# Attention scores as plain fp32 products on the two row halves of TensorE

## The chip, the cores and the metric

The kernel runs on one core of one Trainium2 chip. The metric is the device time in microseconds (us) of one execution; the time before is the median of three runs, 2792.22 us (2788.95 to 2793.67).

## What is computed

The reference is a trunk of two layers over 1024 latent tokens and 256 context tokens, 1024 channels wide, 16 heads of 64. Layer 0 mixes with a two-dimensional neighbourhood attention that has a learned relative-position bias; layer 1 with a sliding window (radius 128), four key-value heads for sixteen query heads, rotary positions and a sink logit for each head. In both a latent query sees its latent neighbours and all 256 context keys in one softmax. A gated convolutional feed-forward follows each. What matters here is the attention:

```
q = rmsnorm(q, g_q);  k = rmsnorm(k, g_k)          # per head of 64
s = einsum('...qngd,...knd->...ngqk', q, k) * 64 ** -0.5   # float32
s = s + bias   (layer 0)      or      where(mask, s, -1e30)   (layer 1)
s = concat([s, sink])         (layer 1)
o = einsum('...ngqk,...knd->...qngd', softmax(s), v)
x = x + gate * (o @ w_out)
```

Everything is fp32 at the inputs and the output.

## The kernel before

**Precision.** Most products run in the single-pass type fp32r. To keep accuracy an operand is split into a rounded part ("hi") and the rest ("lo"), and hi·hi, lo·hi and hi·lo are summed; this is how the projections (`mm`, `oacc`) and the feed-forward (`ua`, `uc`, `dn`) are computed. Products of probabilities and values (`pv`) and the transposes of probabilities (`pt<-idr,S`) are plain fp32.

**Stages.** The modulation and norms of layer 0 come first (to about 60 us), then attention of layer 0 (to about 640 us) with its output projection, then the feed-forward of layer 0 (about 790 to 1620 us), attention of layer 1 (about 1626 to 2060 us) with its projection, and the feed-forward of layer 1. The change touches the two attention stages.

**The order of the work.** Class `Sched` (line 61) is a planner that runs on the host. Each operation is put in with its engine (or a choice of two), an estimated duration, what it reads and writes, a key (smaller is more urgent) and the buffers that it takes (`acq`) and gives back (`rel`). The planner walks through time, gives each free engine its most urgent operation that is ready and whose buffers are free, and so fixes the order of issue on each engine; on the chip every engine then works through its list in that order. Buffers of a kind come free in the order in which they were taken. `CAPS` (line 1002) holds the number of each.

**Layer 0.** For each of 8 pairs of heads `plan_na_qkv` (line 1033) treats 10 tiles of 128 tokens, the two context tiles first: 24 products of 384 columns give queries, keys and values of both heads, which are normed; for each two tiles four plain transposes bring q and k of both heads, 128 rows by 512 columns, into one `pt` bank (line 1073). Then, head by head, 64 rows at a time, the split operands are built (lines 1083 to 1119): `qhi` and `khi` on ScalarE, `qlo` and `klo` on VectorE, and a copy of the keys' two parts to the other 64 rows. So 128 rows of the array hold for one head the query's hi on one half and its lo on the other, beside the same key part on both halves: one product over `kk` gives (hi+lo)·k_hi, a second over `kl` adds (hi+lo)·k_lo.

**Layer 1.** `plan_sw_qkv` (line 2176) does the same for 4 groups of four query heads and one key head: norm, rotary (`qa`, `qb`, `qs`), then the split (`kd`, `klo`, `qhi`, `qlo`, lines 2235 to 2255) into `st` and `klt`, two transposes of the key parts and four of the queries into `pt` banks, and their evacuations by ScalarE.

**Scores and softmax.** `plan_su` (line 571) treats two units of 128 queries: in layer 0 two query tiles of one head (called for head e = 0 and 1 with keys n and n + 1), in layer 1 two heads of one query tile. `qkc` puts the context scores of both units into one `s` bank, 256 columns each, with two products each; `qkl` puts the latent scores of one unit (256 or 384 columns) into another. VectorE reads the context part (`ctx_part`, negated, with a running minimum), then the latent part with bias or mask (`lat_part`); ScalarE takes the exponentials; VectorE or ScalarE scales; TensorE transposes the probabilities in blocks of 128 into `pt` banks, which are copied out. `plan_pv` (line 675) multiplies them with the values of two heads, one on each half of the array's columns, for all key blocks into one `pv` bank.

The eight PSUM banks of the attention stages are dealt out as `PSB = dict(s=3, pt=2, mm=2, pv=1)` (line 994). `Oproj` (line 793) is the output projection; `project` accumulates in `mm` banks, and `weights` loads and splits its weights.

Of the kernel before, what the change touches and what calls it, by code (L numbers as in the profile page):

```python
# [213 lines left out]
def trunk_kernel(ctx, tc, xperm, xseq, cc, crow, wmod, wmodt, bmod, gnorm, na_wqkv, na_gqk, na_bias, na_wo,  # L214
# [356 lines left out]
    def plan_su(sc, key, I, units, groups, psa, wk, reads):  # L571
# [12 lines left out]
        def qkl(k):  # L584
            nl = units[k]["nl"]

            def f(e):
                u = J["u", k]
                t = J["sl", k] = psa("s", F32)
                pe.matmul(t[:, :nl], u["q"], u["kk"], start=True, stop=False)  # L590
                pe.matmul(t[:, :nl], u["q"], u["kl"], start=False, stop=True)
            return f

        sc.op("pe", 4 * t_pe(256), qkc, reads=reads, writes=[K("sc")], key=key, acq=[("s", K("sc"), 2)],
              rel=units[0]["rel_c"] + units[1]["rel_c"])
        for k in range(2):
            if units[k]["nl"]:
                sc.op("pe", 2 * t_pe(units[k]["nl"]), qkl(k), reads=reads + [K("sc")], writes=[K("sl", k)], key=key,
                      acq=[("s", K("sl", k), 1)], rel=units[k]["rel_l"])
        for k in range(2):  # L600
            nl, sink = units[k]["nl"], units[k]["sink"]
            n = TC + nl

            def ctx_part(e, k=k):
                u = J["u", k]
# [4 lines left out]
                dve.tensor_scalar(out=J["S", k][:, :TC], in0=J["sc"][:, k * 256:k * 256 + 256], scalar1=-1.0,  # L610
                                  scalar2=u["sink"] if u["sink"] is not None else 3e38, op0=ALU.mult, op1=ALU.min,
                                  accum_out=J["m", k][:, 0:1])
            sc.op("dve", 0.36, ctx_part, reads=[K("sc")], writes=[K("Sc", k)], key=key,
                  acq=[("S", K("S", k), uses[k])], rel=[K("sc")])
            parts = [K("Sc", k)]
            if nl:
                def lat_part(e, k=k, nl=nl):
                    dve.tensor_tensor_reduce(out=J["S", k][:, TC:TC + nl], in0=J["sl", k][:, :nl], in1=J["u", k]["mask"],
                                             scale=-1.0, scalar=J["m", k][:, 0:1], op0=ALU.add, op1=ALU.min,
                                             accum_out=J["m", k][:, 1:2])  # L620
                sc.op("dve", 0.1 + nl * 0.0012, lat_part, reads=[K("sl", k), K("Sc", k)] + units[k]["mask_key"],
                      writes=[K("Sl", k)], key=key, rel=[K("sl", k)] + units[k]["mask_key"])
                parts.append(K("Sl", k))
# [51 lines left out]
    def plan_pv(sc, key, I, halves, psa, put, ok, acq):  # L675
# [7 lines left out]
        def mm(e):  # L683
            B["pv"] = psa("pv", F32)
# [11 lines left out]
        sc.op("pe", 0.25 + cols * 4 / 2400.0 + 0.02 * n, mm, reads=ps_ + vks, writes=[pk], key=key, acq=[("pv", pk, 1)], rel=ps_ + vks)  # L696
# [96 lines left out]
    class Oproj:  # L793
# [47 lines left out]
        def project(self, dt, key, parts, evac):  # L841

            sc, n = self.sc, self.n
            I = ("oa", dt)
            for kt in range(KT):
                def mm(e, kt=kt):
                    if kt == 0:
                        self.acc[dt] = self.psa("mm", F32)
                    ks = slice(kt * P, (kt + 1) * P)
                    hi, lo = self.ot[self.c]  # L850
                    for i, (w, o) in enumerate(((0, hi), (0, lo), (1, hi))):
                        pe.matmul(self.acc[dt][:, :n], self.w[dt][w][:, ks], o[:, kt, :], start=(kt == 0 and i == 0),
                                  stop=(kt == KT - 1 and i == 2))
                sc.op("pe", 3 * t_pe(n), mm, reads=[("woh", dt), ("wol", dt)] + parts[kt] + self.gate, writes=[I], key=key,
                      acq=[("mm", I, 1)] if kt == 0 else (), rel=[("wo", dt)])
# [138 lines left out]
    PSB = dict(s=3, pt=2, mm=2, pv=1)  # L994
# [6 lines left out]
    SBUFS, PTB = 5, dict(pt5=6, pt2=4, qsq=2)  # L1001
    CAPS = dict(PSB, raw=3, w=WBUFS, S=SBUFS, **PTB, qraw=2, qn=2, qa=2, qb=2, st=2, klt=2,
# [6 lines left out]
    kkl = fin.tile([P, 2, T], F32R, name="kkl")  # L1009
    kll = fin.tile([P, 2, T], F32R, name="kll")  # L1010
# [8 lines left out]
    sc = Sched(dict(CAPS, q=4, qc=1, crow0=1))  # L1019
# [13 lines left out]
    def plan_na_qkv(n):  # L1033
# [9 lines left out]
        def cp(e):  # L1043
            J["raw"] = wk.tile([P, 384], F32, tag="qraw", name="qraw", bufs=2)
# [17 lines left out]
        def qn(e):  # L1062
            if tt % 2 == 0:
                f["qn", pr] = wk.tile([P, 2, 256], F32, tag="qn", name="qn", bufs=2)
# [12 lines left out]
        sc.op("pe", 0.44, tr, reads=[two + (0,), two + (1,)], writes=[K("pt")], key=key, acq=[("pt", K("pt"), 8)], rel=[two])  # L1077
        kx = ("kkc", hp) if cx else ("kk", pr)
        kl = ("klc", hp) if cx else ("kl", pr)
        qx = ("q", hp, pr)  # L1080
        half = [slice(0, DH), slice(DH, P)]

        def qt():
            return f["q"][pr]

        def kt_(lo):
            return f["klc" if lo else "kkc"] if cx else (kll if lo else kkl)[:, :, (tt - 1) * P:(tt + 1) * P]

        def alloc():
            f["q"][pr] = fin.tile([P, 2, 256], F32R, tag="qc" if cx else "q", name="q", bufs=1 if cx else 4)  # L1090
            if cx:
                f["kkc"], f["klc"] = [fin.tile([P, 2, TC], F32R, tag=t, name=t, bufs=2) for t in ("kkc", "klc")]
        for x in range(2):
            a, b = half[x], half[1 - x]

            def qhi(e, x=x, a=a):
                if x == 0:
                    alloc()
                act.activation(qt()[a, x, :], J["pt"][a, 0:256], AF.Copy, scale=gg[a, 2:3])

            def khi(e, x=x, a=a):
                act.activation(kt_(0)[a, x, :], J["pt"][a, 256:512], AF.Copy)

            def qlo(e, x=x, a=a, b=b):
                dve.scalar_tensor_tensor(out=qt()[b, x, :], in0=J["pt"][a, 0:256], scalar=gg[a, 2:3],
                                         in1=qt()[a, x, :].bitcast(F32), op0=ALU.mult, op1=ALU.subtract)

            def klo(e, x=x, a=a):
                ENG[e].tensor_tensor(out=kt_(1)[a, x, :], in0=J["pt"][a, 256:512], in1=kt_(0)[a, x, :].bitcast(F32),
                                     op=ALU.subtract)  # L1110

            def other(lo):
                def f_(e, x=x, a=a, b=b):
                    copy(e, kt_(lo)[b, x, :], kt_(lo)[a, x, :].bitcast(F32))
                return f_
            first = [qx + (0, 0)] if x else []
            sc.op("act", t_actp(256), qhi, reads=[K("pt")] + first, writes=[qx + (x, 0)], key=key,
                  acq=([("qc" if cx else "q", qx, 4 if cx else 8)] + ([("kkc", kx, 20), ("klc", kl, 20)] if cx else []))
                  if x == 0 else (), rel=[K("pt")])
            sc.op("act", t_actp(256), khi, reads=[K("pt"), qx + (0, 0)], writes=[kx + (x, 0)], key=key, rel=[K("pt")])  # L1120
            both = [K("pt"), qx + (x, 0), kx + (x, 0)]
            sc.op("dve", t_dve(256), qlo, reads=both, writes=[qx + (x, 1)], key=key, rel=[K("pt")])
            sc.op("dve", t_dve(256), klo, reads=both, writes=[kl + (x, 0)], key=key, rel=[K("pt")])
            for lo, kk in ((0, kx), (1, kl)):
                sc.op(("act", "dve"), (t_act(256), 0.13 + 256 / 1920.0), other(lo), reads=[kk + (x, 0)], writes=[kk + (x, 1)],
                      key=key)
# [4 lines left out]
    def plan_na_su(n):  # L1131
# [4 lines left out]
        I = ("su0", hp, su, e)  # L1136
# [9 lines left out]
        reads = [t + (e, z) for t in (("kkc", hp), ("klc", hp), ("q", hp, su)) for z in range(2)]  # L1146
        for k in range(2):
# [3 lines left out]
            def get(tt=tt, ch=ch):  # L1151
                u = dict(q=f["q"][su][:, e, tt % 2 * P:(tt % 2 + 1) * P], kkc=f["kkc"][:, e, :], klc=f["klc"][:, e, :], sink=None)
                if tt < 8:
                    ks = slice(ch[0] * P, (ch[-1] + 1) * P)
                    u["kk"], u["kl"] = kkl[:, e, ks], kll[:, e, ks]
# [3 lines left out]
            units.append(dict(nl=len(ch) * P, sink=0, get=get, rel_c=[("q", hp, su), ("kkc", hp), ("klc", hp)],  # L1159
                              rel_l=[("q", hp, su)],  # L1160
                              mask_key=[("bias", hp, e, (0, 0, 1, 1, 1, 1, 2, 2)[tt])] if tt < 8 else []))
            reads += [(n, c // 2, e, z) for c in ch for n in ("kk", "kl") for z in range(2)]
# [17 lines left out]
        f["half", su, e] = plan_su(sc, key, I, units, groups, psa, wk, reads)  # L1180
# [53 lines left out]
    def plan_oproj0():  # L1234
# [12 lines left out]
        def evac(dt, I):  # L1247
            def load(e):
                xin[dt] = wk.tile([P, 384], F32, tag="qraw", name="cx", bufs=2)
# [918 lines left out]
    kkl1 = fin.tile([P, T], F32R, name="kkl1")  # L2168
# [350 lines left out]
```

## Time and profile before

| | |
|---|---|
| median of three runs | 2792.22 us |
| the profiled execution: its time, its span | 2790.61 us, 2788.8 us |
| granted clock of TensorE, mean | 0.990 |
| instructions | 43317 |
| fp32r score products (`s`) | 1088 |
| value products (`pv`), instructions | 1376 |
| transposes of probabilities (`pt<-idr,S`) | 1280 |
| transposes of split queries and keys in layer 1 (`st`, `klt`) | 208 |

In the rows of the profile PE is TensorE's products, PEld its weight loads, DVE VectorE, ACT ScalarE, POOL GpSimd and SP the queue of DMAs. A row of a group has the line, engine, operation, what is written and read, the shapes, the count, then the busy time in us with the mean in ns, and the idle time before the group's instructions with what ended it. All of the kernel's instructions go through one recording helper, so that every row says L51, and the names of the tiles tell the groups apart. `128*64` is the part of the array used, rows by columns. A row of the order in time has the start, the length, the operation and how many were merged. The products are pipelined and their ends modelled: a row's length holds some 0.17 us of latency, and what a product costs its successor is the distance of the starts.

### The profile page before, as it was taken

How to read it: one execution, taken by the hardware profiler on the slowest of the kernel's cores; microseconds unless marked ns; L12 is line 12 of the kernel's file. 1: busy time of each engine (PE TensorE's matmuls, PEld its weight loads, DVE VectorE, ACT ScalarE, POOL GpSimd, SP SyncE). 2: the span in 40 equal slices, each digit the busy share in tenths (PEclk: the TensorE clock that was granted, in tenths of full speed). 3: DMA queues.
4: the chain of work that ended last, by engine and by line, in shares of the span. 5: the costliest groups of instructions: out<-in, count | busy, mean ns of one | idle time of the engine just before them, and what ended most of it. 6: DMA issues, size and time to landing. Idle time of an engine off the chain costs nothing.

```text
span 2788.8 us, 43317 instructions
## 1 busy us (share of the span) xinstructions
PE 2710.8 (97%) x15496; PEld 2331.8 (84%) x15496; DVE 2290.1 (82%) x5040; ACT 1703.7 (61%) x3111; POOL 383.1 (14%) x550
## 2 busy tenths in 40 slices
PE   6999999998999999999999999999998999999999
PEld 4899999987799988888888888888877788888887
DVE  7888888887788788778886889889968988888767
ACT  5677777776455555656564557677754666566433
POOL 2111111112000000000010035656620000000000
PEclk9999999999999999999999999999999999999999
DMA  7233343325555543333475642223243223324655
GB/s 259 85 124 121 118 134 112 112 97 171 209 174 187 175 147 118 113 129 121 151 243 169 205 138 64 75 87 105 88 152 106 80 102 110 106 92 158 232 171 188
DMA packets 148463, 385.30 MB, mean 138 GB/s; under 512 B 21396, under 2 KB 34196, under 8 KB 147864
## 3 DMA queue, kind: packets, MB, share of 16 engines
q1 hardware_dynamic: 148248, 382.55, 41.3%
q8 instruction: 121, 1.98, 0.3%
q14 instruction: 94, 0.77, 0.1%
HBM read 315.50 MB, written 66.99 MB: 137 GB/s over the span
## 4 chain that ended last, share of the span: by engine, by line
PE 83%; DVE 6%; issue 3%; POOL 2%; ACT 1%; DMA 1%; POOLq 0%; DVEq 0%; ACTq 0%
PE ua L51 17%; PE dn L51 15%; PE mm L51 15%; PE uc L51 13%; PE pt L51 5%; PE pv L51 5%; PE s L51 4%; PE ud L51 4%; PE oacc L51 3%; PE dnc L51 2%; DVE S L51 1%; DVE wlo L51 1%; DVE x L51 1%; POOL qa L51 0%; ACT S L51 0%
## 5 line engine op out<-in xcount | busy, mean ns | idle before, releaser
L51 ACT ACTIVATE whi<-wraw 128x512 fp32r<-128x512 f32 (+1 forms) x264 | 212.0, 803 | 152.8 <-PE uc L51 57.4
L51 DVE TENSOR_TENSOR wlo<-wraw,whi 128x512 fp32r<-128x512 f32 (+1 forms) x264 | 240.7, 912 | 47.3 <-ACT whi L51 46.8
L51 ACT ACTIVATE S<-S,m 128x640 f32<-128x640 f32 (+3 forms) x288 | 221.0, 768 | 57.7 <-DVE m L51 39.3
L51 PE MATMUL dn<-ghi,whi 128*128 128x512 f32 x616 | 240.2, 390 | 0.0
L51 PE MATMUL dn<-ghi,wlo 128*128 128x512 f32 x616 | 239.9, 390 | 0.0
L51 PE MATMUL dn<-glo,whi 128*128 128x512 f32 x616 | 239.9, 389 | 0.0
L51 ACT ACTIVATE whi<-s 128x1024 fp32r<-128x1024 f32 (+1 forms) x120 | 113.2, 943 | 193.0 <-PE uc L51 117.9
L51 POOL TENSOR_TENSOR qy<-qv,mhalf 128x4 f32<-128x4 f32 (+2 forms) x120 | 136.7, 1139 | 546.4 <-DVE qv L51 512.7
L51 PE MATMUL pt<-idr,S 128*128 128x128 f32 x1280 | 189.8, 277 | 7.8 <-DVE S L51 3.3
L51 ACT ACTIVATE ghi<-graw 128x512 fp32r<-128x512 f32 x154 | 96.0, 629 | 150.3 <-PE dn L51 96.2
L51 PE MATMUL mm<-whi,h0hi 128*128 128x384 f32 x512 | 181.0, 354 | 1.6 <-ACT qraw L51 1.6
L51 PEld LDWEIGHTS pt<-idr,S 128*128 128x128 f32 x1280 | 151.6, 142 | 26.9 <-issue 9.9
L51 PE MATMUL mm<-wlo,h0hi 128*128 128x384 f32 x512 | 172.7, 337 | 0.0
L51 DVE TENSOR_TENSOR glo<-graw,ghi 128x512 fp32r<-128x512 f32 x154 | 106.2, 698 | 81.0 <-ACT ghi L51 48.4
L51 ACT ACTIVATE pt<-pt 128x512 f32<-128x512 f32 (+2 forms) x241 | 124.5, 536 | 56.6 <-PE pt L51 55.1
L51 PE MATMUL pv<-pt,v 128*64 128x256 f32 (+1 forms) x1376 | 154.7, 371 | 0.0
L51 DVE TENSOR_TENSOR wlo<-s,whi 128x1024 fp32r<-128x1024 f32 (+1 forms) x120 | 129.8, 1081 | 23.3 <-ACT whi L51 23.0
L51 PE MATMUL ua<-t12hi,whi 128*128 128x512 f32 x352 | 139.1, 395 | 4.9 <-ACT t12hi L51 4.7
L51 PE MATMUL uc<-t34h,whi 128*128 128x512 f32 x352 | 139.7, 397 | 0.5 <-ACT t34h L51 0.5
L51 PE MATMUL ua<-t12lo,whi 128*128 128x512 f32 x352 | 138.6, 394 | 1.4 <-DVE t12lo L51 1.4
L51 PE MATMUL uc<-t34l,whi 128*128 128x512 f32 x352 | 137.9, 392 | 0.9 <-DVE t34l L51 0.9
L51 PE MATMUL ua<-t12hi,wlo 128*128 128x512 f32 x352 | 138.1, 392 | 0.0
(325 smaller groups left out, 8527.5 us busy)
## 6 DMA issues: line engine op xcount, KB each, us to landing
wraw<-in_w_up_dram SPq DMA_DIRECT2D x132, 512.0 KB, 3.7
wmt<-in_wmodt_dram SPq DMA_DIRECT2D x96, 512.0 KB, 3.8
wraw<-in_w_down_dram SPq DMA_DIRECT2D x44, 512.0 KB, 3.7
graw<-g_dram SPq DMA_DIRECT2D x44, 512.0 KB, 4.5
wraw<-in_w_down_dram SPq DMA_DIRECT2D x88, 256.0 KB, 3.0
graw<-g_dram SPq DMA_DIRECT2D x66, 256.0 KB, 2.8
wm<-in_wmod_dram SPq DMA_DIRECT2D x32, 512.0 KB, 8.3
slab<-in_na_wqkv_dram SPq DMA_DIRECT2D x32, 384.0 KB, 3.1
```

The source lines that it names most:

```text
L51: r = f(*a, **k)
```

## The change

The scores are computed as plain fp32 products of q and k over the 64 rows of a head. Two heads lie on rows 0 to 63 and 64 to 127, each with a bank of its own for its result. The hi and lo parts of queries and keys are gone, with the operations that made them. In layer 0 q and k of two heads are each copied out of the transposition bank by one operation over 128 rows (`qev`, `kev`), and either ScalarE or VectorE may do it; the two heads' scores are issued together at e = 0. In layer 1 the rotated queries and the doubled key are transposed directly (three transposes a latent tile, one a context tile). Latent keys have two sets of buffers, for alternate pairs or groups. The banks become s = 4, taken two by two, pt = 2 and mm = 2; the value products take a `pt` bank, and the output projection's accumulators, but for the first, the `s` banks once the last scores of the stage are out. With the room that is won the rings of `S`, `q`, `qraw`, `qn` and `qa` are deeper. In layer 1 the load of output weights from the fifth on also waits for the loads of the attention output.

```diff
-    def plan_su(sc, key, I, units, groups, psa, wk, reads):
+    def plan_qk(sc, key, I, get, nl, psa, reads, rel):
+        J = {}
+
+        for t, x, n in (("sc", "kkc", TC), ("sl", "kk", nl)):
+            def mm(e, t=t, x=x, n=n):
+                for h in range(2):
+                    J[t, h] = psa("s", F32)
+                u = get()
+                for h in range(2):
+                    a = slice(h * DH, h * DH + DH)
+                    pe.matmul(J[t, h][:, :n], u["q"][a], u[x][a], start=True, stop=True)
+            out = [I + (t, h) for h in range(2)]
+            if n:
+                sc.op("pe", 0.1 + n * 4 / 2400.0, mm, reads=reads, writes=out, key=key, acq=[("s", x, 1) for x in out],
+                      rel=rel if t == "sc" and not nl or t == "sl" else [])
+        return J, I
+
+    def plan_su(sc, key, I, units, groups, psa, wk):
...
-        def qkc(e):
-            J["sc"] = psa("s", F32)
-            for k in range(2):
-                u = J["u", k] = units[k]["get"]()
-                o = J["sc"][:, k * 256:k * 256 + 256]
-                pe.matmul(o, u["q"], u["kkc"], start=True, stop=False)
-                pe.matmul(o, u["q"], u["klc"], start=False, stop=True)
...
-                pe.matmul(t[:, :nl], u["q"], u["kk"], start=True, stop=False)
-                pe.matmul(t[:, :nl], u["q"], u["kl"], start=False, stop=True)
...
-            B["pv"] = psa("pv", F32)
+            B["pv"] = psa("pt", F32)
...
+            self.s_gate = [("qk0", HP - 1, 3, 1, "sc", 0)] if l == 0 else [("su1", NKV - 1, 7, 1, "sc", 0)]
...
+            tag = "s" if dt else "mm"
...
-                        self.acc[dt] = self.psa("mm", F32)
+                        self.acc[dt] = self.psa(tag, F32)
...
-    PSB = dict(s=3, pt=2, mm=2, pv=1)
+    PSB = dict(s=4, pt=2, mm=2)
...
-    SBUFS, PTB = 5, dict(pt5=6, pt2=4, qsq=2)
+    SBUFS, PTB = 8, dict(pt5=6, pt2=4, qsq=2)
...
-    kkl = fin.tile([P, 2, T], F32R, name="kkl")
-    kll = fin.tile([P, 2, T], F32R, name="kll")
+    kkl = fin.tile([P, 2, T], F32, name="kkl")
...
-    sc = Sched(dict(CAPS, q=4, qc=1, crow0=1))
+    sc = Sched(dict(CAPS, q=5, qc=2, crow0=1))
...
+        def qev(e):
+            f["q"][pr] = fin.tile([P, 256], F32, tag="qc" if cx else "q", name="q", bufs=2 if cx else 5)
+            if e == "act":
+                act.activation(f["q"][pr], J["pt"][:, 0:256], AF.Copy, scale=gg[:, 2:3])
+            else:
+                dve.tensor_scalar(out=f["q"][pr], in0=J["pt"][:, 0:256], scalar1=gg[:, 2:3], scalar2=None, op0=ALU.mult)
+
+        def kev(e):
             if cx:
-                f["kkc"], f["klc"] = [fin.tile([P, 2, TC], F32R, tag=t, name=t, bufs=2) for t in ("kkc", "klc")]
...
+                f["kkc"] = fin.tile([P, TC], F32, tag="kkc", name="kkc", bufs=2)
+            copy(e, f["kkc"] if cx else kkl[:, hp % 2, (tt - 1) * P:(tt + 1) * P], J["pt"][:, 256:512])
...
+        if e == 0:
+            for k in range(2):
...
+                f["qk", su, k] = plan_qk(sc, key, ("qk0", hp, su, k), ops, len(ch) * P, psa,
+                                         [("kkc", hp), ("q", hp, su)] + [("kk", hp % 2, c // 2) for c in ch],
+                                         [("q", hp, su), ("kkc", hp)])
...
+    SBUFS = 7
+    sc = Sched(dict(CAPS, pt2=3, qsq=1, q=10, S=SBUFS))
...
+        def tr(e):
+            J["pt"] = psa("pt", F32)
+            a = J["a"].rearrange("p h d -> p (h d)")
+            for i in range(0 if lat else 2, 3):
+                pe.transpose(J["pt"][:, i * P:(i + 1) * P], a[:, i * P:(i + 1) * P], idf)
...
+        Q = plan_qk(sc, key, I, lambda: dict(q=f["q"][j][:, pr, :], kkc=f["kkc"], kk=kkl1[:, g % 2, ks]), nl, psa,
+                    [("q", g, j), ("kkc", g)] + [("kk", g % 2, t) for t in range(lo, hi + 1)], [("q", g, j), ("kkc", g)])
...
-            op1.weights(dt, sw_wo[dt % KT], OKEY + dt, KT)
+            op1.weights(dt, sw_wo[dt % KT], OKEY + dt, KT, [("oraw", 0, 5)] if dt >= WBUFS else ())
```

More of the change, by code (lines that the diff above doesn't have):

```diff
@@ L1093, in plan_na_qkv @@
[L1093 to L1126, printed above, removed]
@@ L1151, in get @@
             def get(tt=tt, ch=ch):
[L1152 removed]
+                u = dict(sink=None)
                 if tt < 8:
[L1154 to L1155 removed]
                     bb, o = ((0, 0), (0, 256), (1, 0), (1, 0), (1, 0), (1, 0), (2, 0), (2, 384))[tt]
@@ L1158, in get @@
                 return u
-            units.append(dict(nl=len(ch) * P, sink=0, get=get, rel_c=[("q", hp, su), ("kkc", hp), ("klc", hp)],
-                              rel_l=[("q", hp, su)],
+            units.append(dict(nl=len(ch) * P, sink=0, get=get, s=f["qk", su, k] + (e,),
                               mask_key=[("bias", hp, e, (0, 0, 1, 1, 1, 1, 2, 2)[tt])] if tt < 8 else []))
-            reads += [(n, c // 2, e, z) for c in ch for n in ("kk", "kl") for z in range(2)]
         def val(c):
@@ L1178, in plan_na_su @@
         ok = ("osb", hp, su)
-        f["half", su, e] = plan_su(sc, key, I, units, groups, psa, wk, reads)
+        f["half", su, e] = plan_su(sc, key, I, units, groups, psa, wk)
         if e == 0:
@@ L2258, in trk @@
-        def trk(e):
-            J["pt2"] = psa("pt", F32R)
-            pe.transpose(J["pt2"][:, 0:P], J["st"][:, 4, :], idr)
-            pe.transpose(J["pt2"][:, P:2 * P], J["klt"].rearrange("p x d -> p (x d)"), idr)
-        sc.op("pe", 0.21, trk, reads=[K("kd"), K("kl")], writes=[K("pt2")], key=key, acq=[("pt", K("pt2"), 2)],
-              rel=[K("klt"), K("st")] + ([] if lat else [K("st")]))
-        kk, kl = (("kk", tt), ("kl", tt)) if lat else (("kkc", g), ("klc", g))
-        first = [] if lat or tt == ORDER[0] else [kk, kl]
+                J["a"] = wk.tile([P, 6, DH], F32, tag="qa", name="qa", bufs=3)
@@ L2267, in kev @@
+        sc.op("pe", 0.11 * (3 if lat else 1), tr, reads=[K("a")], writes=[K("pt")], key=key,
+              acq=[("pt", K("pt"), 2 if lat else 1)], rel=[K("a")])
+        kk = ("kk", g % 2, tt) if lat else ("kkc", g)
+        first = [] if lat or tt == ORDER[0] else [kk]
         def kev(e):
             if tt == ORDER[0]:
-                f["kkc"] = fin.tile([P, TC], F32R, tag="kkc", name="kkc", bufs=2)
-            dst = kkl1[:, tt * P:(tt + 1) * P] if lat else f["kkc"][:, (tt - 8) * P:(tt - 7) * P]
@@ L2271, in kev @@
-            copy(e, dst, J["pt2"][:, 0:P].bitcast(F32))
-        sc.op("act", t_actp(128), kev, reads=[K("pt2")] + first, writes=[kk], key=key,
-              acq=[("kkc", kk, 32)] if tt == ORDER[0] else (), rel=[K("pt2")])
-        def lev(e):
-            if tt == ORDER[0]:
-                f["klc"] = fin.tile([P, TC], F32R, tag="klc", name="klc", bufs=2)
-            dst = kll1[:, tt * P:(tt + 1) * P] if lat else f["klc"][:, (tt - 8) * P:(tt - 7) * P]
-            copy(e, dst, J["pt2"][:, P:2 * P].bitcast(F32))
@@ L2280, in plan_sw_qkv @@
-        sc.op("act", t_actp(128), lev, reads=[K("pt2")] + first, writes=[kl], key=key,
-              acq=[("klc", kl, 32)] if tt == ORDER[0] else (), rel=[K("pt2")])
-        if lat:
-            def trq(e):
-                J["pt"] = psa("pt", F32R)
-                for i in range(4):
-                    pe.transpose(J["pt"][:, i * P:(i + 1) * P], J["st"][:, i, :], idr)
-            sc.op("pe", 0.43, trq, reads=[K("qh"), K("ql")], writes=[K("pt")], key=key, acq=[("pt", K("pt"), 1)],
-                  rel=[K("st")])
+                f["kkc"] = fin.tile([P, TC], F32, tag="kkc", name="kkc", bufs=2)
```

143 lines of the change are left out of this document (56 added, 87 removed).

## Prediction

> **What bounds the kernel now.** I read the page first, then the busy time of each engine in the two attention stages (layer 0 from about 60 to 640 us, layer 1 from 1626 to 2058 us), then what TensorE waited for there.
>
> ```profile
> span 2788.8 us, 43317 instructions
> PE 2710.8 (97%) x15496; PEld 2331.8 (84%) x15496; DVE 2290.1 (82%) x5040; ACT 1703.7 (61%) x3111; POOL 383.1 (14%) x550
> PE 83%; DVE 6%; issue 3%; POOL 2%; ACT 1%; DMA 1%; POOLq 0%; DVEq 0%; ACTq 0%
> ```
>
> The chain of waits is TensorE for 83% of the span. The windows (length, then busy time of PE, PEld, DVE, ACT, POOL) say the same of the stages that the change touches:
>
> ```profile
> 100.00:600.00 500.00, 497.85 (x3426) 456.96 (x3424) 438.71 (x1541) 372.01 (x877) 75.23 (x67) 1.00 0.38 121
> 1660.00:2000.00 340.00, 330.51 (x2413) 292.36 (x2413) 309.80 (x1045) 251.69 (x617) 204.23 (x367) 0.99 0.24 75
> 600.00:700.00 100.00, 90.17 (x630) 78.94 (x630) 73.50 (x215) 64.10 (x135) 23.34 (x17) 0.97 0.46 150
> 2000.00:2100.00 100.00, 95.97 (x550) 76.80 (x547) 71.41 (x179) 55.74 (x107) 33.10 (x49) 0.98 0.42 143
> ```
>
> In layer 0 TensorE is idle 2.2 of 500 us, in layer 1 9.5 of 340, and in the two tails, where the output projections begin, 9.8 and 4.0. That is 25.5 us in all, and its clock is full (1.00, 0.99). So time on TensorE counts one for one, and work saved on VectorE and ScalarE counts only through those 25.5 us and some shorter gaps that the modelled ends cover.
>
> **Scores, their streaming time.** Today each head's scores are two products per key block (keys and their low parts):
>
> ```profile
> L51 PE MATMUL s<-kkc,q 128*128 128x256 f32 x288 | 82.3, 307 | 0.8 <-DVE S L51 0.7
> L51 PE MATMUL s<-klc,q 128*128 128x256 f32 x288 | 75.7, 284 | 2.0 <-ACT klc L51 2.0
> L51 PE MATMUL s<-kkl,q 128*128 128x384 f32 x192 | 72.1, 376 | 5.9 <-DVE m L51 3.8 <-DVE S L51 1.6
> L51 PE MATMUL s<-kll,q 128*128 128x384 f32 x192 | 65.7, 342 | 0.0
> L51 PE MATMUL s<-kkl,q 128*128 128x256 f32 x64 | 18.8, 303 | 0.0
> L51 PE MATMUL s<-kll,q 128*128 128x256 f32 x64 | 17.5, 282 | 0.0
> ...
> 403.59 0.28 PE L51 MATMUL s<-kkc,q 128*128 128x256 f32 x1
> ...
> 404.06 0.34 PE L51 MATMUL s<-kkl,q 128*128 128x384 f32 x1
> 404.23 0.34 PE L51 MATMUL s<-kll,q 128*128 128x384 f32 x1
> 404.41 0.33 PE L51 MATMUL mm<-whi,h0chi 128*128 128x384 f32 x1
> ```
>
> The means hold the pipeline's latency, so I price by starts: four products of 256 columns lie between 403.59 and 404.06, 0.1175 each; two of 384 lie between 404.06 and 404.41, 0.175 each. 704 x 0.1175 + 384 x 0.175 = 149.9 us.
>
> What a plain fp32 product costs, and two of them on two halves of the array, is seen in the products of probabilities and values, which are plain fp32 and lie on the two column halves:
>
> ```profile
> L51 PE MATMUL pv<-pt,v 128*64 128x256 f32 x1184 | 144.2, 386 | 0.0
> L51 PE MATMUL pv<-pt,v 128*64 128x128 f32 x192 | 15.9, 273 | 0.0
> ...
> 1680.56 1.88 PE pv L51 x16
> 1693.10 2.31 PE pv L51 x20
> ```
>
> The code has 592 and 96 of these products, so each is two instructions. In the chain of waits a block of 256 columns more, for two heads (4 instructions), makes a run 0.43 us longer, so a pair on two halves takes 0.43 for 256 columns and 0.645 for 384 (by columns). The new scores are 176 pairs of 256 (144 of context, 32 of latent keys) and 96 of 384: 176 x 0.43 + 96 x 0.645 = 137.6 us. **That saves 12.3.** On streaming alone four passes for two heads at once are nearly what four single passes were.
>
> **What going to and from half the array costs.** This is the term that decides. Here is one such run of values among full-array products:
>
> ```profile
> 411.14 0.34 PE L51 MATMUL mm<-whi,h0clo 128*128 128x384 f32 x1
> 411.31 0.34 PE L51 MATMUL mm<-wlo,h0chi 128*128 128x384 f32 x1
> 411.58 2.17 PE L51 MATMUL pv<-pt,v 128*64 128x256 f32 x20
> 413.68 0.39 PE L51 MATMUL s<-kkc,q 128*128 128x256 f32 x1
> 413.90 0.28 PE L51 MATMUL s<-klc,q 128*128 128x256 f32 x1
> ```
>
> The last full product has its 0.17 until 411.48. The second score starts at 413.90, so the first would, at its usual 0.12, have started at 413.78: 2.30 us for the run. Its stream is four pairs of 256 columns and one of 128, 4 x 0.43 + 0.215 = 1.94. So 0.36 us go on entering and leaving: neither the array nor the weight load runs ahead across the change. The scores are full-array products today and pay none of it. A score's weights are 128 columns wide where a value's are 64:
>
> ```profile
> L51 PEld LDWEIGHTS pv<-pt,v 128*64 128x64 f32 x1376 | 91.5, 137 | 53.2 <-issue 14.2 <-ACT kkl L51 0.2
> L51 PEld LDWEIGHTS s<-klc,q 128*128 128x128 f32 x288 | 55.4, 192 | 2.2 <-ACT klc L51 2.2
> ```
>
> The exposed first load is thus 0.055 longer: **0.41 us a visit.** No row shows row halves, so the bounds are 0 (entering is free; below zero there is nothing to gain, as the streams are priced apart) and 0.47 (the two halves' first loads one behind the other, 0.055 more). I take 0.41, since the value run is the only half-array work in the trace.
>
> The Trainium skill, page "TensorEngine Tiling (Array Packing)", section "Key Properties", says that changing the tiling mode, not merely the tile, drains the TensorE; for column halves the trace agrees (0.36 us), for row halves no run here shows it. By that rule the sum below stays; without it the visits cost nothing and the sum is the first rival's.
>
> **How many visits.** Four banks hold two pairs. In layer 0 (32 units of two latent query tiles and 8 of context) the first tile's context and latent pairs can go together. The second tile's context pair needs both banks of the first, and the second of these comes free only when VectorE has read the second head's part; the latent pair's banks come free one latent reduction later. So I count three visits a latent unit (bounds 2 and 4) and one a context unit (bounds 1 and 2): 104, from 72 to 144. In layer 1 there are 64 units of two pairs, in one visit or two: 80, from 64 to 128. **184 x 0.41 = 75.4 us** (136 x 0.36 = 49 to 272 x 0.47 = 128; 0 if free).
>
> **Transposes.** Layer 1 loses 208 transposes of the split parts and gains 104 plain ones (three a latent tile, one a context tile):
>
> ```profile
> L51 PE MATMUL pt<-idr,st 128*128 128x128 f32 x168 | 25.1, 246 | 3.6 <-POOL st L51 2.6 <-DVE pt L51 0.7
> L51 PE MATMUL pt<-idr,klt 128*128 128x128 f32 x40 | 9.9, 246 | 2.2 <-DVE klt L51 1.3 <-POOL klt L51 0.6
> ...
> 1660.08 0.45 PE L51 MATMUL pt<-idr,st 128*128 128x128 f32 x4
> 1660.37 0.40 PE L51 MATMUL mm<-whi,h1hi 128*128 128x384 f32 x1
> ...
> 408.41 1.04 PE L51 MATMUL pt<-idr,S 128*128 128x128 f32 x8
> 409.20 0.42 PE L51 MATMUL mm<-whi,h0chi 128*128 128x384 f32 x1
> ```
>
> Four of the old take 0.29 to the next start, eight plain ones 0.79: 208 x 0.073 = 15.2 against 104 x 0.099 = 10.3, **4.9 saved**. Layer 0's transposes stay.
>
> **What leaves the other engines.** In layer 0 ten evacuations and copies of 64 partitions for each pair of tiles become two of 128 partitions; in layer 1 the split of queries and keys goes. The largest rows, the first four from 100 to 600 us and the last from 1660 to 2000:
>
> ```profile
> L51 DVE SCALAR_TENSOR_TENSOR q<-pt,gg,q 64x256 fp32r<-64x256 f32 x68 | 32.9, 483 | 22.1 <-ACT q L51 17.1 <-ACT kkl L51 1.9 <-ACT kkc L51 0.7
> L51 DVE TENSOR_TENSOR kll<-pt,kkl 64x256 fp32r<-64x256 f32 x53 | 22.4, 422 | 4.6 <-ACT kkl L51 4.0
> L51 ACT ACTIVATE q<-pt,gg 64x256 fp32r<-64x256 f32 x67 | 31.3, 467 | 8.5 <-PE pt L51 7.7
> L51 ACT ACTIVATE kkl<-kkl 64x256 fp32r<-64x256 f32 x53 | 22.1, 417 | 1.3
> ...
> L51 POOL TENSOR_TENSOR st<-qa,st 128x256 fp32r<-128x256 f32 x29 | 22.7, 783 | 11.9 <-ACT st L51 10.5 <-DVE pt L51 1.3
> ```
>
> That is over 100 us of VectorE and ScalarE time in that window, yet it is beside TensorE, so it can only close TensorE's gaps. Of the 25.5 us idle I take **20 saved** (bounds 0 and 40, as gaps under a pipeline's tail are not in the 25.5). The deeper rings (S, q, qraw, qn, qa) and the two sets of latent keys serve the same gaps and are priced there. What would be late next is the score banks: a pair waits for two of four, and on TensorE's in-order stream whatever product follows waits with it. The planner puts projection products ahead of a pair that isn't due, and these are the cover; after the last of them (628 to 641 us, 2005 to 2058) there is none. Values now share the two transposition banks, 72 runs in all; at worst some ten runs without that cover wait half a microsecond each, 5 us. I take 0. Moving the later output weights of layer 1 behind the reloads on SP's queue, and the projection's accumulators to the score banks, lies in the 2000 to 2100 window, whose idle 4.0 us bounds a gain; at worst one load is late, about 4 us. I take 0.
>
> **Sum.** -12.3 - 4.9 + 75.4 - 20 = +38 us on the profiled execution's 2790.6 us, whose span is 2788.8; the median of three, 2792.2, is 1.6 above it. Forecast **2830 us**, slower by 1.4%. This case's own range: 2800 (the fewest visits at 0.36, -12 - 5 + 49 - 20 = +12, a little under it for larger gaps closed) to 2880 (about 90 more: 250 visits at 0.47, gaps hardly closed).
>
> **Rivals.** First, row halves are entered without a drain, or nearly. For it: the two row halves keep all 128 output columns, so nothing changes at the array's outputs. Against it: 0.36 us at each value run. Then -12 - 5 - 20 = -37, 2755 us; at 0.1 a visit, 2774. It decides below (37 / 184 =) 0.20 us a visit. Chance 0.27, and this is the side on which the kernel becomes faster. Second, the fp32 products of the two row halves don't run side by side: the streams double, 138 us more, 2968 us. Against it: the value pairs do so on column halves. Chance 0.06. Third, visits join to about 136 and the closed gaps reach 30 us: -12 - 5 + 49 - 30 = +2, no change. Chance 0.09; for it the gaps in layer 1, against it the banks' order above.
>
> **How the numbers follow.** The main case has 0.58 and is slower; with the second rival slower is 0.64, faster 0.27, same 0.09. Within 0.2%, some 5.6 us, nothing is told from no change. The range takes in the main case and most of the first rival: 2762 to 2880.
>
> **What would show it.** Right: score products of 64 rows, two instructions each, the second half starting with the first; about 138 us of score stream; each visit about 0.4 us longer than its stream; 136 to 272 visits; layer 0 longer by 15 to 45 us and layer 1 by 0 to 25; idle time of TensorE under 10 us in the four windows. Wrong: a full-array product that starts at its usual distance behind a score pair (then the first rival), or the halves' starts one product apart (the second).

## The result and the profile after

The changed kernel takes 2807.49 us (median of four runs, 2805.52 to 2808.49) against 2791.59 us (four runs, 2788.95 to 2793.67): ratio 1.0057, 95% interval 1.0039 to 1.0074. That is 16 us slower: the direction was forecast, the size (38 us) was not. The profiled execution is 17.7 us longer in its span. The page of the changed kernel:

```profile
span 2806.5 us, 42574 instructions
PE 2748.6 (98%) x15392; PEld 2262.1 (81%) x15392; DVE 2193.7 (78%) x4839; ACT 1599.9 (57%) x2786; POOL 337.6 (12%) x524
PE 91%; DVE 3%; DMA 2%; issue 2%; POOL 1%; ACT 1%; SPq 0%; POOLq 0%; DVEq 0%; ACTq 0%
```

VectorE is 96 us less busy, ScalarE 104, and the chain is TensorE for 91% in place of 83%. The same four windows, in the same columns:

```profile
100.00:600.00 500.00, 500.00 (x3319) 416.27 (x3320) 365.47 (x1343) 300.57 (x684) 69.77 (x65) 1.00 0.37 119
1660.00:2000.00 340.00, 338.70 (x2285) 254.41 (x2286) 291.00 (x1026) 218.25 (x490) 179.98 (x350) 1.00 0.24 75
600.00:700.00 100.00, 92.99 (x642) 76.09 (x639) 68.91 (x214) 60.06 (x128) 15.80 (x13) 0.95 0.42 135
2000.00:2100.00 100.00, 96.04 (x543) 68.44 (x539) 72.96 (x200) 60.08 (x119) 29.20 (x55) 0.97 0.37 122
```

TensorE's idle time there is 12.3 us (0 + 1.3 + 7.0 + 4.0), where it was 25.5 before. Where the time went is read from three products whose first start marks a stage. The rows by tile give shortest, median and longest duration in ns, then the first and last start; first before the change, then after:

```profile
L51 PE MATMUL uc<-h2chi,whi x352: 277/283/365, 786.6 to 974.8; 128*128 128x256 f32 x176
L51 PE MATMUL mm<-whi,h1chi x64: 220/275/416, 1625.9 to 1917.1; 128*128 128x128 f32 x64
L51 PE MATMUL ua<-b1hi,whi x88: 387/390/506, 2134.9 to 2557.3; 128*128 128x512 f32 x88
```

```profile
L51 PE MATMUL uc<-h2chi,whi x352: 278/283/365, 794.6 to 984.3; 128*128 128x256 f32 x176
L51 PE MATMUL mm<-whi,h1chi x64: 220/279/416, 1635.1 to 1929.9; 128*128 128x128 f32 x64
L51 PE MATMUL ua<-b1hi,whi x88: 389/389/498, 2152.7 to 2575.1; 128*128 128x512 f32 x88
```

Layer 0's attention with its projection ends 8.0 us later (794.6 against 786.6). Layer 1's takes 517.6 us (1635.1 to 2152.7) against 509.0, 8.6 more. The feed-forwards stay within about a microsecond. The scores and the plain transposes of layer 1:

```profile
L51 PE MATMUL s<-kkc,q 64*128 64x256 f32 x576 | 100.8, 426 | 0.1
L51 PE MATMUL s<-kkl,q 64*128 64x384 f32 x384 | 87.4, 519 | 2.8 <-DVE m L51 2.8
L51 PE MATMUL s<-kkl,q 64*128 64x256 f32 x128 | 21.0, 405 | 0.0
L51 PE MATMUL pt<-idr,qa 128*128 128x128 f32 x104 | 19.3, 286 | 1.8 <-POOL qa L51 1.7
```

Each product is two instructions on 64 rows, as foreseen. One visit to the 64-row mode, in the order in time:

```profile
407.69 0.33 PE L51 MATMUL mm<-wlo,h0hi 128*128 128x384 f32 x1
407.95 0.70 PE L51 MATMUL s<-kkc,q 64*128 64x256 f32 x4
408.49 0.81 PE L51 MATMUL s<-kkl,q 64*128 64x384 f32 x4
409.23 0.45 PE L51 MATMUL mm<-whi,h0chi 128*128 128x384 f32 x1
409.51 0.34 PE L51 MATMUL mm<-whi,h0clo 128*128 128x384 f32 x1
```

The product before it has its 0.17 until 407.86; the second one behind it starts at 409.51, so the first would undisturbed have started at 409.34. The visit takes 1.48 us, its stream 0.43 + 0.645 = 1.075. The remaining 0.40 is the price forecast (0.41). Unrounded it is 0.406 in the median of 42 visits that lie between undisturbed products. The heads' four instructions need the time of two, so they run side by side.

**An account of TensorE's time.** For each kernel I added up, over the two layers' stages (62 us to the first `uc`, first `mm<-whi,h1chi` to the next `ua`), what each product costs its successor when nothing disturbs it (the start distances of the prediction), 0.354 us for each value run, 0.406 for each visit, and 0.2 less where the two adjoin. What is left of the stage's length is gaps, also those that the modelled ends cover, and also what is lost while the granted clock is down. The absolute gaps carry the error of these prices; I use their differences.

| | visits | streams | value runs and visits | gaps, layer 0 + 1 |
|---|---|---|---|---|
| before | 0 | 1128.8 | 25.5 | 36 + 43 = 79 |
| after | 199 | 1111.9 | 100.3 | 16 + 21 = 37 |

Streams fell by 16.9 us (scores 12.8, transposes 4.1), visits added 74.8, and 41 us of gaps closed: +16.5, against 8.0 + 8.6 measured. So the prices held in the sum, and the closing of gaps was mis-sized. The experiments ask what closed them.

The theory: 41 us of gaps closed because the other engines lost work and because added TensorE time falls partly into time in which it waited. Rivals: the deeper rings or the second set of keys closed them; or the visits cost less in all than their sum.

### The profile page after: what moved, and what is told of

The parts are those of the page before. It is cut to its first block, busy times and chain, and to the rows that moved or that the text cites. A ratio compares the mean times of both kernels' runs of the same rounds, so it can differ in the third digit from the quotient of the medians.

```text
span 2806.5 us, 42574 instructions
## 1 busy us (share of the span) xinstructions
PE 2748.6 (98%) x15392; PEld 2262.1 (81%) x15392; DVE 2193.7 (78%) x4839; ACT 1599.9 (57%) x2786; POOL 337.6 (12%) x524
## 4 chain that ended last, share of the span: by engine, by line
PE 91%; DVE 3%; DMA 2%; issue 2%; POOL 1%; ACT 1%; SPq 0%; POOLq 0%; DVEq 0%; ACTq 0%
PE mm L51 18%; PE ua L51 17%; PE dn L51 15%; PE uc L51 13%; PE pt L51 12%; PE s L51 8%; PE ud L51 4%; PE oacc L51 3%; PE dnc L51 2%; DMA wm<-in_wmod_dram 1%; DVE x L51 1%; DVE wlo L51 0%; DMA slab<-in_na_wqkv_dram 0%; PE mod L51 0%; POOL qb L51 0%
## 5 line engine op out<-in xcount | busy, mean ns | idle before, releaser
L51 ACT ACTIVATE S<-S,m 128x641 f32<-128x641 f32 (+4 forms) x288 | 220.3, 766 | 79.0 <-DVE m L51 65.4
L51 ACT ACTIVATE pt<-pt 128x512 f32<-128x512 f32 (+2 forms) x275 | 140.8, 528 | 93.9 <-PE pt L51 92.7
L51 PE MATMUL mm<-whi,h0hi 128*128 128x384 f32 x512 | 187.0, 365 | 0.0
L51 PE MATMUL pt<-pt,v 128*64 128x256 f32 (+1 forms) x1376 | 154.2, 370 | 0.0
```

Of the source, the lines that this page charges most:

```text
L51: r = f(*a, **k)
```

## Experiments

**The changed kernel without visits** (`full`).

```diff
-                    a = slice(h * DH, h * DH + DH)
-                    pe.matmul(J[t, h][:, :n], u["q"][a], u[x][a], start=True, stop=True)
+                    for i in range(2):
+                        pe.matmul(J[t, h][:, :n], u["q"], u[x], start=i == 0, stop=i == 1)
-    kkl = fin.tile([P, 2, T], F32, name="kkl")
+    kkl = fin.tile([P, 2, T], F32R, name="kkl")
...
```

The tiles `kkl1`, `kkc` and `q` become F32R likewise.

> The changed kernel, but each head's scores are two fp32r products over all 128 rows (as many columns streamed as before the change, 149.9 us in place of 137.6), so that TensorE never goes to 64 rows. The scores then mix the two heads: the output is not the reference's, and only the time is read. Theory A (visits cost what was forecast, 75 us, and the gaps that closed were larger than forecast): 2807 - 75 + 12 = about 2745 us. Rival C (the visits cost less in all than forecast, about 55 us, because some lie where TensorE would have waited anyway): 2765 us or more.

2758.75 us (2754.47 to 2762.57), 0.9882 of before (0.9869 to 0.9896): 49 us under the changed kernel, where 62 was expected (2745 us): the time lies between the two forecasts. With the same score stream as before and no visit, everything else of the change is worth 33 us. Its gaps are 18 + 33 = 51 us: 28 closed, not 41. The other 13 opened again when TensorE got faster. Its windows show it: in the same 340 us of layer 1 TensorE is idle for 10.6 us where it is 1.3 in the changed kernel, while VectorE is busier (306 us against 291).

```profile
100.00:600.00 500.00, 500.00 (x3472) 463.13 (x3472) 376.84 (x1388) 311.14 (x714) 71.85 (x67) 1.00 0.38 123
1660.00:2000.00 340.00, 329.36 (x2389) 288.48 (x2388) 306.34 (x1078) 235.79 (x526) 188.47 (x358) 0.99 0.28 87
```

**The same with full-array work added** (`fullpad`).

```diff
+                    pe.matmul(J[t, h][:, :256], u["q"], u[x][:, :256], start=True, stop=True)
                     for i in range(2):
```

> The kernel of the run full with one fp32r product of 256 columns more for each head of each score pair: 544 x 0.1175 = 64 us of TensorE work, about what the changed kernel has over the run full (75 - 12 = 63), but in full-array products without any change of mode. As in full the scores are not the reference's. If TensorE's time counts one for one: 2759 + 64 = 2823 us. If part of any added TensorE work falls into time in which it waited, above all in layer 1: 2806 to 2812, as the changed kernel. If the visits themselves cost less than 0.41 each: 2820 or more here, against 2807 there.

2814.22 us (2814.10 to 2814.66): 55 us for 64 us of products. Between the two forecasts: some 9 us fell into waits, 11 by the account (gaps 16 + 24 = 40). So added TensorE time is not paid in full even where it has nothing to do with modes, mostly in layer 1 (33 to 24). That speaks against visits that cost less than 0.406 each; it leaves open the last 4 us.

**Ring depths of before** (`rings`).

```diff
-    SBUFS, PTB = 8, dict(pt5=6, pt2=4, qsq=2)
+    SBUFS, PTB = 5, dict(pt5=6, pt2=4, qsq=2)
...
-    sc = Sched(dict(CAPS, q=5, qc=2, crow0=1))
+    sc = Sched(dict(CAPS, q=4, qc=1, crow0=1))
...
```

In the same way `qraw`, `qn` and `qa` go from 3 to 2, and in layer 1 `S` from 7 to 5 and `q` from 10 to 7.

> The changed kernel with the ring depths of before (S 5, qraw, qn and qa 2, q 4 and 7, the context q 1). Theory A (the gaps closed because the split work left the other engines): within 5 us of the changed kernel, 2807 to 2812. Rival B (the deeper rings closed them): 10 to 25 us slower, 2817 to 2832.

2806.12 us (2803.36 to 2808.37), 1.0051 of before (1.0037 to 1.0064): no difference from the changed kernel. The deeper rings are no cause there.

**One set of latent keys** (`fullkeys`, on `full`).

```diff
-            copy(e, f["kkc"] if cx else kkl[:, hp % 2, (tt - 1) * P:(tt + 1) * P], J["pt"][:, 256:512])
+            copy(e, f["kkc"] if cx else kkl[:, 0, (tt - 1) * P:(tt + 1) * P], J["pt"][:, 256:512])
...
```

Layer 1 is changed likewise.

> The run full with one set of latent keys in place of two, in both layers; the scores are not the reference's, as in full. The load put back gave 19 of 28 us of closed gaps again. If the second set of keys closed the rest: 2764 to 2770 us. If it closed none: within 4 us of 2759.

2759.93 us (2754.59 to 2760.45), 0.9882 of before (0.9867 to 0.9897), as `full`. The second set is no cause either.

**The removed load put back** (`load`, on the changed kernel; `fullload`, on `full`).

```diff
+        for es in ["act"] * 3 + ["dve"] * 3 + [("act", "dve")] * 4:
+            sc.op(es, ..., extra, reads=[two + (0,), two + (1,)], key=key, rel=[two])
+        sc.op("act", t_act(128), extrak, reads=[K("a")], key=key, rel=[K("a")])
+        sc.op("pool", t_pool(128), extrak, reads=[K("a")], key=key, rel=[K("a")])
+        if lat:
+            sc.op("act", t_act(256), extra, ...)
+            sc.op("pool", t_pool(256), extra, ...)
```

The first loop stands in layer 0 for each two tiles, the rest in layer 1 for each tile. Before the change each two tiles of layer 0 have twelve such operations (eight read the bank, four copy the keys' parts to the other rows), after it two; ten copies make the count twelve again. The buffers of `qn` and `qa` are now given back only when the copies have read them.

> The changed kernel with work put back that has no use: for each two tiles of layer 0 ten copies of 64 rows by 256 (three on ScalarE, three on VectorE, four on either), for each tile of layer 1 copies of 128 and 256 columns on ScalarE and GpSimd. Nobody waits for them. Theory A, in the form that the load of the engines made the gaps: 10 to 25 us slower, 2817 to 2832. Rival B: within 5 us. If it was not the load but the length of the chain from projection to queries: within 5 us as well.

> The kernel of the run full with the useless copies of the run load. Same output as full. If the removed work of VectorE, ScalarE and GpSimd is what closed the 26 us of gaps between before and full: 2780 to 2790 us, with layer 0 giving back most of its 18 us. If it was the shorter chain or the second set of keys: layer 0 gives back under 5 us, and the whole is 2760 to 2772.

`load`: 2828.59 us (2826.72 to 2829.65), 21 us slower than the changed kernel; gaps 20 + 35 = 55 for 37, and 6 visits more. `fullload`: 2781.56 us (2779.26 to 2785.20), 23 us of the 33 given back, 19 of them in the two stages. Nobody uses what a copy writes. A later tile could wait for the buffers that it holds, but the trace of `fullload` puts no wait of TensorE's products, VectorE, ScalarE or GpSimd down to a copy. Gaps 24 + 46 = 70: all of what layer 1 had gained, but only 6 of layer 0's 18. Part of layer 1's 13 is a lower granted clock, 0.97 over the stage against 0.99 in `full`; in the next run, whose layer 1 is the same, it is 0.99 again and the stage is 3 us shorter. The first products of the stages in `fullload`:

```profile
L51 PE MATMUL uc<-h2chi,whi x352: 278/283/365, 774.9 to 964.7; 128*128 128x256 f32 x176
L51 PE MATMUL mm<-whi,h1chi x64: 220/275/476, 1615.4 to 1908.8; 128*128 128x128 f32 x64
L51 PE MATMUL ua<-b1hi,whi x88: 389/389/628, 2123.8 to 2548.0; 128*128 128x512 f32 x88
```

Layer 0 ends at 774.9, still 11.7 before the kernel before. The time came out as forecast for load, but layer 0 gave back neither "most of its 18 us" nor under 5. Nor is the load of layer 0 all back. Its stage, from 62 us to the first `uc`, before the change and in `fullload` (columns as above):

```profile
62.00:786.60 724.60, 706.25 (x4626) 638.05 (x4625) 604.60 (x1959) 499.66 (x1126) 106.55 (x92) 0.99 0.39 129
62.00:774.90 712.90, 699.14 (x4626) 638.17 (x4625) 575.78 (x1961) 488.25 (x1126) 107.94 (x91) 0.99 0.41 131
```

VectorE has nearly as many operations as before (1961 for 1959), but is busy for 29 us less (in `full` it is 530 us). So the rest of layer 0 can be load that is still missing, or something else.

**The transposition bank held longer** (`fullhold`, on `fullload`).

```diff
+        for x in range(3):
+            sc.op("act", t_actp(256), hold, reads=[K("pt")], writes=[K("ex", x)], key=key, rel=[K("pt")])
+            sc.op("dve", t_dve(256), hold, reads=[K("pt"), K("ex", x)], key=key, rel=[K("pt")])
-        for es in ["act"] * 3 + ["dve"] * 3 + [("act", "dve")] * 4:
+        for es in [("act", "dve")] * 4:
-              acq=[("pt", K("pt"), 2)]
+              acq=[("pt", K("pt"), 8)]
```

> The run fullload, except that in layer 0 six of the ten useless copies read the transposition bank itself, three on ScalarE and behind each of them one on VectorE, so that the bank is given back after eight readers, as before the change, and not after two. The load is the same. Load put back gave layer 0 only 6 of its 18 us of closed gaps again. If the short hold of the bank closed the other 12: about 2790 us, with layer 0 some 8 to 12 us longer than in fullload. If not: within 4 us of 2782.

2790.02 us (2784.39 to 2794.11), 0.9992 of before (0.9983 to 1.0001), as forecast for the hold. With these copies and readers back, nothing is left of the 33 us that can be told from none. The profiled execution, the shortest of eleven, has its first up-projection at

```profile
L51 PE MATMUL uc<-h2chi,whi x352: 277/283/365, 784.1 to 972.3; 128*128 128x256 f32 x176
```

which is 9.2 us later than in `fullload`, all of it gaps (24 to 33). But the edit moved more than the hold. The same stage again, and the longest wait of VectorE in it (in all, times, longest):

```profile
62.00:784.10 722.10, 707.11 (x4626) 637.88 (x4625) 598.09 (x1978) 473.51 (x1112) 109.89 (x88) 0.99 0.41 130
DVE dump0dve L51 <- ACT dump0act L51: 29.0, 60, 1.1
```

The number of copies is the same, yet VectorE is busy for 22 us more than in `fullload` and ScalarE for 15 less: the planner dealt the operations out anew (1978 for 1961 on VectorE). And the two engines now wait for each other in the chain of readers. By the order in time the bank is held, from the first transpose to the end of its last reader, for 4.0 us in the median of 40, against 4.9 before the change and 1.6 in `full`. So it is held for longer, as meant; but of TensorE's waits in this stage that the trace names, only one, of 0.5 us, is for one of these eight readers. What the hold alone is worth, and what VectorE's fuller time and the chain are, this run doesn't separate.

**Fewer visits** (`join`; `price` and `joinprice` change the planner's price of a visit; `aware` and `joinaware` make the planner know the mode).

```diff
+        def mm(e):
+            u = get()
+            for t, x, n in parts:
...
+        sc.op("pe", 0.1 * len(parts) + (TC + nl) * 4 / 2400.0, mm, reads=reads, writes=out, key=key,
+              acq=[("s", x, 1) for x in out], rel=rel)
...
-                sc.op("pe", 0.1 + n * 4 / 2400.0, mm, ...
+                sc.op("pe", 0.4 + n * 4 / 2400.0, mm, ...
...
+                        d += 0.4 if o["half"] and not was else 0.2 if o["half"] and o["half"] != was else 0.0
```

The first part is `join` (one operation for four banks), the second `price`, the last line `aware`; `joinprice` gives the joined operation 0.4 + (TC + nl) * 4 / 2400.0, and `joinaware` has the first and the last part.

> The changed kernel with the context and latent pair as one operation that takes all four banks, so 136 visits in place of 199. Theory A: 63 x 0.406 = 26 us less, about 2782 us, if the wait for all four banks is covered by projection products. Rival C: 10 to 15 us less. If the four banks at once make TensorE wait: 2800 or more, and the waits show on the score products.

> The changed kernel with a visit priced in the planner at 0.4 us in place of 0.1; only the order of issue changes. If the low price is what keeps TensorE from waiting (it runs behind the plan, the others ahead of it): waits come back, 2815 us or more. If the order is no cause: within 5 us of 2807. If the true price gives a better order, visits joined: 2795 to 2802.

> The run join (136 visits) with the visit priced at 0.4 us. If join's lost 24 us went to waits that come from the plan's wrong time: 2785 to 2798 us. If they come from all four banks being taken at once: within 5 us of join's 2806.

> The changed kernel with a planner that knows the array's mode: a score pair or value run costs 0.4 us more when TensorE comes from full-array products, 0.2 when it comes from the other half mode, and right behind one half-array operation another one that is ready goes first. Planned are 168 visits with 78 changes straight between scores and values, in place of 199 and 30. Theory A: (31 x 0.406 + 48 x 0.2 =) 22 us less TensorE work, of which half to all is seen: 2785 to 2797 us. If visits are no cause: 2802 or more.

> The same planner with context and latent pair as one operation: 136 visits, 63 of the changes straight between scores and values, in place of joinprice's 140 and 31. Theory A: (4 x 0.406 + 32 x 0.2 =) 8 us less than joinprice's 2792: 2783 to 2789 us, faster than both kernels. If the order costs as much in waits: 2790 to 2795.

| | visits, of them next to a value run | time, us | ratio to before, interval | gaps |
|---|---|---|---|---|
| join | 136, 19 | 2805.82 | 1.0049, 1.0037 to 1.0062 | 20 + 39 = 59 |
| price | 206, 42 | 2817.77 | 1.0086, 1.0071 to 1.0101 | 20 + 27 = 47 |
| joinprice | 140, 31 | 2792.10 | 0.9998, 0.9988 to 1.0007 | 13 + 29 = 42 |
| aware | 168, 78 | 2791.95 | 1.0000, 0.9991 to 1.0008 | 16 + 29 = 45 |
| joinaware | 136, 63 | 2793.71 | 1.0004, 0.9995 to 1.0013 | 18 + 37 = 55 |

The visits came as planned and cost as priced, but with the order of issue the gaps moved by as much. `join` saved 23 us of changes of mode by the account (76.9 for 100.3) and lost 22 to gaps (59 for 37). The longest waits of TensorE in its layer 1 (in all, times, longest) are for probabilities, rotated queries and a score reduction:

```profile
PE pt L51 <- DVE S L51: 3.0, 4, 1.6
PE pt L51 <- POOL qa L51: 2.1, 2, 1.9
PE pt L51 <- ACT S L51: 1.7, 2, 0.9
PE s L51 <- DVE m L51: 1.1, 2, 0.9
```

These are the few waits long enough to be seen, 8 of 39 us, and most stand at transposes, where the expectation had the score products. Another part is the clock. Layer 1's stage in the changed kernel, `join` and `joinprice` (columns as above, the granted clock is the third from the end):

```profile
1635.10:2152.70 517.60, 511.92 (x3210) 390.68 (x3209) 422.19 (x1331) 311.96 (x662) 215.33 (x410) 0.99 0.30 98
1631.20:2150.20 519.00, 508.71 (x3209) 401.58 (x3208) 426.05 (x1321) 308.06 (x665) 221.53 (x415) 0.97 0.30 98
1624.60:2133.10 508.50, 498.78 (x3209) 393.44 (x3208) 423.71 (x1323) 311.49 (x669) 213.61 (x410) 0.99 0.32 100
```

`join` has 0.97 where the other two have 0.99. As an estimate from these rows, 0.02 of 519 us is some 10 us, of the 18 by which `join`'s gaps in layer 1 exceed the changed kernel's. It is no accident of one execution, for the mean clock of `join`'s five runs is 0.987 to 0.990, that of the changed kernel's four 0.991 to 0.994. (`aware` has 0.99 in this stage, `joinaware` 0.98.) Whether the clock fell because TensorE waited, no run here shows. With the visit priced right the joined kernel gained 14 us, the unjoined one lost 10: no rule for the order comes out of this, and why is left open. `aware` gave 16 us of the 22 that its visits promised. `joinaware`, which promised 8 under `joinprice`, gave nothing. Here is a visit of `aware` straight behind a value run:

```profile
300.04 0.34 PE L51 MATMUL mm<-wlo,h0hi 128*128 128x384 f32 x1
300.31 2.17 PE L51 MATMUL pt<-pt,v 128*64 128x256 f32 x20
302.41 1.14 PE L51 MATMUL s<-kkc,q 64*128 64x256 f32 x8
303.47 0.44 PE L51 MATMUL mm<-whi,h0hi 128*128 128x384 f32 x1
303.75 0.34 PE L51 MATMUL mm<-whi,h0lo 128*128 128x384 f32 x1
```

From 300.21 to 303.58 are 3.37 us, the streams 1.94 + 0.86 = 2.80 and the changes 0.57: 0.36 for the value run and 0.20 more for the visit, half of what it costs alone. Of the versions with visits three (`joinprice`, `aware`, `joinaware`) can't be told from the kernel before, and none is faster.

## Why the prediction was right in its direction and wrong in its size

- **Streams.** Forecast -12.3 and -4.9; the account has -12.8 and -4.1. Four passes for two heads at once do cost nearly what four single passes did.
- **Visits.** 184 x 0.41 = 75.4 us forecast. There were 199 at 0.406, which is 80.8, and 30 adjoined value runs at 0.2 less each: 74.8. The price was right; that the sum fits to 0.6 us is luck, for layer 0 had 93 visits (104 forecast) and layer 1 106 (80), and the discount beside value runs was not foreseen. The first rival falls by the 0.406 us, the second by the pairs' starts. With the rule of the Trainium skill (page "TensorEngine Tiling (Array Packing)", section "Key Properties"), that a change of the tiling mode drains TensorE, the trace now agrees for row halves too (0.406 us a visit).
- **Gaps: the step that failed.** "Of the 25.5 us idle I take 20 saved (bounds 0 and 40)": the runs show 41, twice that and above the upper bound. First, the term was sized from the idle time of the windows, which counts from the modelled ends: over layer 0's stage (62 to 786.6 us) that is 18.4 us, by the distances of starts some 36. Gaps under a pipeline's tail were named in the prediction, but not counted. Second, the freed time of the other engines was worth more than forecast: of the 28 us that close at an equal score stream the useless copies opened 19 again (`fullload`, though some of it by a lower clock). The other 9 opened again in `fullhold`, with the transposition bank held longer, VectorE 22 us busier and a chain between two engines; which of them it was stays open. The prediction had that bank as a possible loss, because values now share it, and left out that queries and keys give it back after two readers in place of eight. It also counted ten operations that become two; there were twelve. The deeper rings and the second keys, which it put into the same term, gave nothing by themselves. The third, some 13 us, is the next point. What the fourth score bank is worth was not tried by itself.
- **One for one.** "Time on TensorE counts one for one" also failed: 64 us of added products cost 55 (`fullpad`), and the visits' and streams' net 62 us cost 49 (`full` against the changed kernel). Some 13 of the 41 us are this. By the account most of it lies in layer 1 (gaps 33 in `full`, 24 in `fullpad`, 21 in the changed kernel): where TensorE waits for others, a slower TensorE waits less.
- **Sum.** -16.9 + 74.8 - 41.4 = +16.5. With the forecast's own prices and these gaps the time would have been 2809 us. The third rival, no change, had larger closed gaps in mind (30), but too few visits (136).
- **What would show it.** Two instructions, halves starting together, the score stream, the price and the number of visits were right, and so was layer 1 longer by 0 to 25 us (8.6). Layer 0 longer by 15 to 45 us was wrong (8.0), and idle time under 10 us in the four windows was missed (12.3).

## What to carry to other kernels

A product on half the array is priced by its stream and by its visits: count how often the order of issue goes to the half mode and back. Half-mode work side by side costs less (0.20 us in place of 0.41 here), but look at the gaps that the new order makes. Before counting saved work on other engines at nothing because TensorE is busy, count TensorE's gaps by start distances, since busy time with modelled ends hides them. When an experiment is to change one thing, such as how long a bank is held, look in its trace whether the busy time of the other engines stayed. Where a second engine is nearly as busy, as VectorE was in layer 1 (291 to 310 of 340 us), saved or added time on the busiest may not be paid in full.

## What the runs showed of the hardware

- Entering and leaving a 64-row mode with 128-column weights costs 0.406 us among full-array products (median of 42 visits, 0.393 the least), the 64-column mode of the values 0.355; going straight from one to the other costs 0.20 on top of the first (0.555 together, median of 8 in the changed kernel). The difference of 0.05 is about that of one weight load (0.137 and 0.192 us before the change); that it comes from the first weight load was forecast and fits, but was not tested by itself.
- In plain fp32 a product is two instructions, and the two row halves of a pair run side by side: in 532 of the 544 pairs of instructions they start within about 0.01 us of each other.
